# Moving a kernel's gate writes from ScalarE's DMA queue to GpSimd's, spreading gathers over the freed blocks, and loading residual rows later

## The chip, the cores and the metric

One core of a Trainium2 chip. The metric is the device time of one execution in microseconds (us), median over runs. Engines are named as in the profile: PE (TensorE), DVE (VectorE), ACT (ScalarE), POOL (GpSimd), SP (SyncE, which here only issues DMAs). DMAs are issued from three queues: SP's and ACT's (in the profile q1 and q10, "hardware_dynamic") and POOL's (q0, "software_dynamic").

## What is computed

A decoder layer on 1024 tokens of width 1024: a mixer (attention and a diagonal state-space model), cross-attention, and an expert layer. The change touches the expert layer and the final norm alone:

```
q = (h @ w_pq).reshape(b, s, 8, 2, 128)
scores = einsum('bshid,hikd->bshik', q, sub_keys)          # 128 keys per half
half_val, half_idx = top_k(scores, 16)
best_val, best_pos = top_k(all 256 sums, 16)               # 16 experts per head
expert = i1 * 128 + i2                                     # one of 16384
gate = softmax(best_val)
act = einsum('btd,bthkd->bthk', h_blk, peer_u[e_blk])
out = einsum('bthk,bthkd->btd', gate * gelu(act), peer_v[e_blk])
return rmsnorm(h + out, g_final)
```

## The kernel before

Tokens come in 8 blocks of 128 (tb 0 to 7), experts in 128 blocks of 128 (e 0 to 127). Two methods share the work. For tb 3 to 7 (the dense blocks, ND = 5) the kernel multiplies all experts: it needs a dense gate matrix, expert x token, mostly zeros. For tb 0 to 2 it gathers rows of the tables by expert number instead: 128 gathers of 128 rows (512 KB) for each token block and table; tb 2 takes its activations from the dense product and gathers rows of peer_v alone.

**The expert loop** runs e from 0 to 127. `u_load` (L1523) brings 512 KB of peer_u on SP's queue two blocks ahead, `u_hi` (L1529, ACT) and `u_lo` (L1535, DVE) split it into two parts one block ahead, `expert_acts` (L1542) runs 48 matmuls on PE, a GELU on ACT, and writes the result to DRAM with two DMAs on ACT's queue (acm, actd). Into each block other work is put by `plan(e, rank, f)`: all of block e's entries are issued in the order of their rank, and this order is kept by hand on every engine's queue (`in_order`, L1631). `u_hi` has rank -1, `u_lo` and `u_load` 0.5, `expert_acts` 7.

Such work is, first, the **dense gates**. For each dense token block, one after the other with a period of PER = 22 blocks from T0 = 6, the blocks 0 to 16 of the period make the gate matrix in 16 pieces: one-hot rows on DVE (`gate_make`), their scaling on ACT (`gate_power`), 16 small matmuls, and an eviction by ACT into the tile Gs (`gate_mm`, L1505, evicted at L1515). Gs is a single buffer of 64 KB in each partition. `gate_out` (L1517) then writes it to DRAM (gd) in 16 DMAs of 512 KB, each of 8 x 128 pieces of 512 bytes: 4, 3, 3, 3, 3 in the blocks 16 to 20 of the period, rank 4.7, on ACT's queue. The next token block writes Gs again from block 23 on. These five blocks are called a burst here; there are five bursts.

Second, the **gathers**: 384 in the loop. `gather_get` (rank 6) issues one on POOL's queue into one of six buffers, and in the next block (rank 1) `gather_u` (L1319) or `gather_v` (L1334) consumes it on DVE. The list `open_` (L1576) says into which blocks they go, in equal numbers: blocks 13 to 126 without the blocks 17 to 20 of a period, 94 blocks, so four in nearly each and none in the last four blocks of a burst. Third, the **routing** (top-k, expert numbers) of the coming token block, on DVE; in the second and third period two token blocks are routed.

**The last stage** multiplies 32 groups (gi) of four expert blocks. For each expert block `v_load` (L1604) brings a peer_v block, the activations and the gates (vr, vag, gg) on SP's queue into one of two buffers, `v_split` (L1613) scales and splits them on ACT and DVE, and the matmuls of the five dense token blocks (n = 0 to 4) follow. Even n accumulate in PSUM over all groups (`held`), odd n (tb 4 and 6) go through two PSUM buffers that DVE adds to the residual h in every group (`add`, L1670). Gathered rows of tb 1 and 2 are added to h beside it (`take`, L1665). Before the first group, SP's queue gets nine loads: h for all eight token blocks (L1660, 512 KB each) and the final gain (L1662). tb 0, 2, 3, 5 and 7 of h are first used later than the first group.

Of the kernel before, what the change touches and what calls it, by code (L numbers as in the profile page):

```python
# [9 lines left out]
F32 = mybir.dt.float32  # L10
# [13 lines left out]
P = 128  # L24
S = 1024
D = 1024
TB = S // P
# [8 lines left out]
GT_N = 2  # L36
GV_N = 3
# [23 lines left out]
def hybrid_kernel(ctx, tc, x, mem, g_mix, w_in, a_re, a_im, log_dt, b_re, b_im, c_re, c_im, d_skip,  # L61
                  w_glu, b_glu, g_attn, g_ssm, w_out, g_xattn, g_mem, w_xqT, w_xkv, w_xo, g_ffn,
                  g_ffn_row, w_pqT, keysT, peer_uT, peer_u, peer_v, g_final, out, dbg=None, upto=99):
    nc = tc.nc
    V, G = nc.vector, nc.gpsimd
# [897 lines left out]
    with ExitStack() as st:  # L963
# [16 lines left out]
        with ExitStack() as st2:  # L980
# [3 lines left out]
            for th in range(2):  # L984
                t = slice(th * 512, (th + 1) * 512)
# [292 lines left out]
    gd = dr.tile([P, P, TG], F32, name="gd")  # L1278
# [12 lines left out]
    GT, Gs = {}, {}  # L1291
# [14 lines left out]
    def gather(pool, table_ap, tb, k, name, bufs):  # L1306
        r = pool.tile([P, D], F32, name=name, bufs=bufs)
        ins = G.indirect_dma_start(out=r, out_offset=None, in_=table_ap,  # L1308
                                   in_offset=bass.IndirectOffsetOnAxis(ap=gk[tb][0][:, k:k + 1], axis=0))
        return r, ins  # L1310
# [10 lines left out]
    def gather_w(tb):  # L1321
        act(gk[tb][2], gk[tb][2], AF.Gelu_apprx_tanh)
        V.tensor_mul(gk[tb][1], gk[tb][1], gk[tb][2])
# [139 lines left out]
    def plan(e, rank, f):  # L1463
        todo.setdefault(e, []).append((rank, f))
# [34 lines left out]
    def gate_power(tb, b):  # L1499

        o2, power = oneh[tb, b][1], GT[tb][2][0]
        for k in range(8):
            nc.scalar.activation(o2[:, k, :], o2[:, k, :], AF.Copy, scale=power[:, b * 8 + k:b * 8 + k + 1])  # L1503
# [12 lines left out]

    def gate_out(tb, q):  # L1517
        i = slice(q * 8, q * 8 + 8)
        nc.scalar.dma_start(gd[i, :, (tb - GV_N) * P:(tb - GV_N + 1) * P].rearrange("i p t -> p i t"), Gs[tb][:, i, :])

    urows, usplit = {}, {}

# [33 lines left out]
    T0 = 6  # L1556
    PER = 114 // ND
    GSPAN = 16
    R0 = 9
    plan_route(GV_N, 0, 5)  # L1560
    for n in range(ND):
        tb = GV_N + n
        at = T0 + n * PER
        for b in range(16):
            plan(at + b * GSPAN // 16, 0, lambda tb=tb, b=b: gate_make(tb, b))
            plan(at + b * GSPAN // 16, 4.5, lambda tb=tb, b=b: gate_power(tb, b))
            plan(at + b * GSPAN // 16 + 1, 4, lambda tb=tb, b=b: gate_mm(tb, b))
        for q in range(16):
            plan(at + GSPAN + q * 5 // 16, 4.7, lambda tb=tb, q=q: gate_out(tb, q))
        if n + 1 < ND:  # L1570
            r0 = R0 if 0 < n < GV_N else 6
            plan_route(tb + 1, at + r0, PER - 1 - r0)
    for tb in range(GV_N):
        plan_route(tb, T0 + tb * PER, R0 if tb else 6)
    G0 = T0 + 7
    open_ = [e for e in range(G0, P - 1) if (e - T0) % PER not in range(GSPAN + 1, GSPAN + 5)]  # L1576
    V0 = T0 + (ND - 1) * PER + GSPAN + 6

    def v_open():
# [13 lines left out]
    for i, (kind, tb, k) in enumerate(asks):  # L1593
        e = open_[len(open_) * i // len(asks)]
# [58 lines left out]
    with ExitStack() as st:  # L1653
        vpools[1] = st.enter_context(tc.tile_pool(name="vb", bufs=CG, side="right"))
        hp2 = st.enter_context(tc.tile_pool(name="hp2", bufs=1, side="right"))
        psV2 = st.enter_context(tc.tile_pool(name="psV2", bufs=2, space=PSUM))
        psV3 = st.enter_context(tc.tile_pool(name="psV3", bufs=1, space=PSUM))
        h = hp2.tile([P, TB, D], F32, name="hf")
        for tb in range(TB):
            nc.sync.dma_start(h[:, tb, :], h2d[tb])  # L1660
        gfin = hp2.tile([P, D], F32, name="gfin")
        nc.sync.dma_start(gfin, g_final[0:1, :].to_broadcast([P, D]))  # L1662
        got, adds = [], []

        def take(n):  # L1665
            for _ in range(n):
                tb, k, r = got.pop(0)
                V.scalar_tensor_tensor(h[:, tb, :], r, gk[tb][1][:, k:k + 1], h[:, tb, :], op0=OP.mult, op1=OP.add)  # L1668

        def add(n):  # L1670
            for _ in range(n):
                tb, d, pv = adds.pop(0)
                V.tensor_add(h[:, tb, d], h[:, tb, d], pv)  # L1673

        def finish(tb):
            ss = hp2.tile([P, 1], F32, name="ss", bufs=2)
            sq = va_raw.tile([P, D], F32, name="vr")
            nc.scalar.activation(sq, h[:, tb, :], AF.Square, accum_out=ss)
            r = rsqrt_mean(hp2, ss, 1, D, "no")
            V.scalar_tensor_tensor(h[:, tb, :], h[:, tb, :], r, gfin, op0=OP.mult, op1=OP.mult)  # L1680
            nc.sync.dma_start(out[tb * P:(tb + 1) * P, :], h[:, tb, :])

        NG = P // CG
        STEPS = ND
        turn = {math.floor(STEPS * i / CG): i for i in range(CG)}

        held = {n: [psV3.tile([P, 512], F32, name=f"acc{n}{nh}") for nh in range(2)] for n in range(0, STEPS, 2)}
        flat = acm.rearrange("a b (t o) -> (a b t) o", o=1)

        def ask(i):  # L1690

            tb, k = GT_N - 1 + i // P, i % P
            if i < P:
                G.indirect_dma_start(out=gk[GT_N][2][:, k:k + 1], out_offset=None, in_=flat,
                                     in_offset=bass.IndirectOffsetOnAxis(ap=gidx[:, k:k + 1], axis=0))
            if i == P:
                V.tensor_mul(gk[GT_N][1], gk[GT_N][1], gk[GT_N][2])
            got.append((tb, k, gather(hp2, peer_v, tb, k, "rv", 6)[0]))

        NK = (GV_N - GT_N + 1) * P  # L1700
        asked = 0
        with in_order():
            for gi in range(NG):
                for n in range(STEPS):
                    tb = GV_N + n
                    low = None
                    if n in turn and gi + 1 < NG:
                        e = (gi + 1) * CG + turn[n]
                        low = v_split(e)
                        if e + 2 < P:  # L1710
                            v_load(e + 2)
                    if gi == 0 and n == 0:
                        gather_w(GT_N - 1)
                    want = min(NK, NK * (gi * STEPS + n + 1) // ((NG - 1) * STEPS))
                    if len(got) > 3:
                        take(len(got) - 3)
                    while asked < want:
                        if len(got) > 5:
                            take(1)
                        ask(asked)  # L1720
                        asked += 1
                    t = slice(n * P, (n + 1) * P)
                    for nh in range(2):
                        d = slice(nh * 512, nh * 512 + 512)
                        keep = n in held
                        pv = held[n][nh] if keep else psV2.tile([P, 512], F32, name="pv")
                        first, last = not keep or gi == 0, not keep or gi == NG - 1
                        for k, (wh, wl, vh, vl) in enumerate(groups[gi]):
                            mm3(pv, (wh[:, t], wl[:, t]), (vh[:, d], vl[:, d]), first and k == 0, last and k == CG - 1)
                        if last:  # L1730
                            adds.append((tb, d, pv))
                    if n and gi == NG - 1:
                        add(2)
                        finish(tb - 1)
                    else:
                        add(len(adds) - 2 * (n not in held or gi == NG - 1))
                    if low:
                        low()
                groups.pop(gi)
                if gi == NG - 2:  # L1740
                    take(len(got))
                    for tb in range(GV_N):
                        finish(tb)
            tb = TB - 1
            parts = hp2.tile([P, 2], F32, name="parts")
            for k in range(2):
                d = slice(k * 512, k * 512 + 512)
                add(1)
                sq = va_raw.tile([P, D], F32, name="vr")
                nc.scalar.activation(sq[:, d], h[:, tb, d], AF.Square, accum_out=parts[:, k:k + 1])  # L1750
            ss = hp2.tile([P, 1], F32, name="ss", bufs=2)
            V.tensor_add(ss, parts[:, 0:1], parts[:, 1:2])
            r = rsqrt_mean(hp2, ss, 1, D, "no")
            for k in range(2):
                d = slice(k * 512, k * 512 + 512)
                V.scalar_tensor_tensor(h[:, tb, d], h[:, tb, d], r, gfin[:, d], op0=OP.mult, op1=OP.mult)
                nc.sync.dma_start(out[tb * P:(tb + 1) * P, d], h[:, tb, d])
# [57 lines left out]
```

## Time and profile before

| | us |
|---|---|
| median of 3 runs | 3324.71 (3318.75 to 3328.46) |
| profiled execution, its own time | 3330.65 |
| its span | 3328.5 |
| PE busy | 3140.5 (94%) |
| DVE busy | 2554.3 (77%) |
| ACT busy | 1271.5 (38%) |
| POOL busy | 1282.9 (39%) |

Stages: the expert loop runs from 1141 to 2420 us of the span, the last stage from there to the end. How to read the rows below. In a table of stretches: the stretch A:B in us from the span's start and its length, then for PE, PEld (weight load), DVE, ACT and POOL the busy time (and number of instructions), then PE's granted clock as a share of full speed, the mean busy share of the 16 DMA engines, and what they moved in GB/s. The share is a sum of packet durations and can pass 1 a little where packets overlap. In a timeline: start, duration, engine, line, operation, out<-in, count, and in brackets how long the engine was idle before and what ended that. In a view of one line or tile: duration in ns as minimum/median/maximum, then first and last start. In groups of instructions: busy us, mean ns of one | idle time before them and what ended it. An engine's name with a q (ACTq, SPq) is its queue of DMA issues; these do not count as busy.

### The profile page before, as it was taken

The page shows a single profiled execution, that of the slowest core. Times are in us where ns is not written, and L with a number is a line of the kernel's source. Part 1 is how long each engine was busy: PE and PEld are TensorE (multiplying, and loading weights), DVE is VectorE, ACT ScalarE, POOL GpSimd, SP SyncE. Part 2 cuts the span into 40 slices and gives each one's busy share as a digit, 9 for nine tenths or more (in the row PEclk, how much of TensorE's full clock was granted, in tenths as well). Part 3 has the DMA queues.
Part 4 walks back from the last instruction along what each step waited for, and adds up shares of the span by engine and source line. Part 5 has one row for each costly group of instructions (what it writes and reads, how often), then busy time and mean ns, then how long its engine had stood idle before and what let it go on. Part 6 is the DMA issues. An engine that isn't in the chain of part 4 may idle for free.

```text
span 3328.5 us, 46822 instructions
## 1 busy us (share of the span) xinstructions
PE 3140.5 (94%) x16767; PEld 2617.7 (79%) x16767; DVE 2554.3 (77%) x5041; ACT 1271.5 (38%) x2405; POOL 1282.9 (39%) x1099
## 2 busy tenths in 40 slices
PE   7999998999999899998889898999889999999998
PEld 7987675787888688777778787888768888888787
DVE  8356888364588689699699697894768888888887
ACT  3215655154421156365355364562222222222222
POOL 4233545100000005255245254452557777544442
PEclk9999999999999899999999999999989999999999
DMA  5336543531220238988888899899989999898895
GB/s 177 90 91 215 174 136 105 183 114 51 89 92 1 76 105 285 305 271 278 304 269 294 302 329 329 302 332 352 345 309 325 337 334 331 327 341 318 321 335 203
DMA packets 362280, 788.83 MB, mean 237 GB/s; under 512 B 41408, under 2 KB 160704, under 8 KB 358848
## 3 DMA queue, kind: packets, MB, share of 16 engines
q0 software_dynamic: 105056, 356.63, 30.7%
q1 hardware_dynamic: 136928, 336.93, 29.1%
q10 hardware_dynamic: 120064, 92.30, 8.5%
q8 instruction: 131, 2.15, 0.3%
q14 instruction: 101, 0.83, 0.1%
HBM read 649.97 MB, written 135.76 MB: 236 GB/s over the span
## 4 chain that ended last, share of the span: by engine, by line
PE 57%; DVE 19%; issue 10%; DMA 6%; ACT 3%; POOL 2%; ACTq 2%; SPq 1%; DVEq 0%; POOLq 0%
PE pu L1548 12%; DVE ru L1319 4%; PE acc L163 4%; PE acc L162 4%; PE acc L164 4%; PE pp L164 4%; PE pp L162 4%; PE pp L163 4%; DMA gg<-gd 3%; PE pv L162 3%; PE pv L163 3%; PE pv L164 3%; PE pq L162 2%; PE pq L163 2%; PE pq L164 2%
## 5 line engine op out<-in xcount | busy, mean ns | idle before, releaser
L1548 PE MATMUL pu<-hTh,uh 128*128 128x512 f32 (+1 forms) x2048 | 544.1, 347 | 56.9 <-ACT uh L1532 56.8
L1308 POOL DMA_INDIRECT ru<-in_peer_u_dram,ge x256 | 353.8, 1382 | 524.1 <-DVE ru L1319 341.9
L1548 PE MATMUL pu<-hTh,ul 128*128 128x512 f32 (+1 forms) x2048 | 535.4, 343 | 6.3 <-DVE ul L1539 6.3
L1548 PE MATMUL pu<-hTl,uh 128*128 128x512 f32 (+1 forms) x2048 | 534.9, 343 | 0.0
L1308 POOL DMA_INDIRECT rv<-in_peer_v_dram,ge x256 | 361.2, 1411 | 306.5 <-DVE hf L1668 250.9
L1548 PEld LDWEIGHTS pu<-hTh,uh 128*128 128x128 f32 x2048 | 321.2, 193 | 103.7 <-ACT uh L1532 60.8
L1548 PEld LDWEIGHTS pu<-hTh,ul 128*128 128x128 f32 x2048 | 319.9, 192 | 54.7 <-DVE ul L1539 8.5
L1548 PEld LDWEIGHTS pu<-hTl,uh 128*128 128x128 f32 x2048 | 319.8, 192 | 46.2
L1668 DVE SCALAR_TENSOR_TENSOR hf<-rv,gg,hf 128x1024 f32<-128x1024 f32 x256 | 327.7, 1280 | 3.6
L1539 DVE TENSOR_TENSOR ul<-ur,uh 128x1024 fp32r<-128x1024 f32 x128 | 156.3, 1221 | 199.6 <-ACT uh L1532 183.6
L1319 DVE SCALAR_TENSOR_TENSOR ru<-ru,hn 128x1024 f32<-128x1024 f32 x256 | 305.2, 1223 | 1.8 <-DMA ru<-in_peer_u_dram,ge 1.8
L162 PE MATMUL acc<-vh,wh 128*128 128x512 f32 x768 | 298.8, 389 | 0.9 <-issue 0.9
L164 PE MATMUL acc<-vh,wl 128*128 128x512 f32 x768 | 298.8, 389 | 0.0
L163 PE MATMUL acc<-vl,wh 128*128 128x512 f32 x768 | 298.8, 389 | 0.0
L1618 ACT CAST vh<-vr 128x1024 fp32r<-128x1024 f32 x128 | 134.7, 1052 | 363.3 <-PE acc L164 178.1
L1308 POOL DMA_INDIRECT ru<-in_peer_v_dram,ge x128 | 160.9, 1257 | 238.5 <-DVE hf L1334 190.2
L88 ACT ACTIVATE ag<-pu 128x512 f32<-128x512 f32 (+1 forms) x256 | 110.8, 484 | 345.8 <-PE pu L1548 239.0
L1503 ACT ACTIVATE o<-o,power 128x128 bf16<-128x128 bf16 x640 | 194.1, 388 | 104.5 <-DVE o L1492 76.3
L162 PE MATMUL pv<-vh,wh 128*128 128x512 f32 x512 | 201.7, 394 | 20.0 <-DVE hf L1673 20.0
L1621 DVE TENSOR_TENSOR gg<-gg,vag 128x640 f32<-128x640 f32 x128 | 105.8, 826 | 142.6 <-DMA gg<-gd 130.7
L1622 ACT CAST wh<-gg 128x640 fp32r<-128x640 f32 x128 | 93.3, 729 | 303.6 <-DVE gg L1621 254.5
L164 PE MATMUL pv<-vh,wl 128*128 128x512 f32 x512 | 200.7, 392 | 0.0
(496 smaller groups left out, 6931.3 us busy)
## 6 DMA issues: line engine op xcount, KB each, us to landing
ur<-in_peer_uT_dram SPq DMA_DIRECT2D x128, 512.0 KB
vr<-in_peer_v_dram SPq DMA_DIRECT2D x128, 512.0 KB
actd<-ag ACTq DMA_DIRECT2D x128, 320.0 KB
gd<-Gs ACTq DMA_DIRECT2D x80, 512.0 KB
vag<-actd SPq DMA_DIRECT2D x128, 320.0 KB
gg<-gd SPq DMA_DIRECT2D x128, 320.0 KB
qk<-qkd POOLq DMA_DIRECT2D x16, 768.0 KB
wr<-in_w_in_dram SPq DMA_DIRECT2D x8, 1024.0 KB
```

Source lines behind the costliest of these rows:

```text
L88: ins = nc.scalar.activation(o, i, func, **kw).ins
L162: nc.tensor.matmul(out_ap, lh, rh, start=first, stop=False, **kw)
L163: nc.tensor.matmul(out_ap, lh, rl, start=False, stop=False, **kw)
L164: nc.tensor.matmul(out_ap, ll, rh, start=False, stop=last, **kw)
L1308: ins = G.indirect_dma_start(out=r, out_offset=None, in_=table_ap, in_offset=bass.IndirectOffsetOnAxis(ap=gk[tb][0][:, k:k + 1], axis=0))
L1319: V.scalar_tensor_tensor(r, r, 1.0, hn[tb], op0=OP.mult, op1=OP.mult, accum_out=gk[tb][2][:, k:k + 1])
L1503: nc.scalar.activation(o2[:, k, :], o2[:, k, :], AF.Copy, scale=power[:, b * 8 + k:b * 8 + k + 1])
L1539: V.tensor_sub(ul, urows.pop(e), uh.bitcast(F32))
L1548: nc.tensor.matmul(pu[th][:, :b - a], w[:, dc, :], r_[:, dc, a:b], start=f, stop=l)
L1618: nc.scalar.copy(vh, vr)
L1621: V.tensor_mul(gg, gg, ag)
L1668: V.scalar_tensor_tensor(h[:, tb, :], r, gk[tb][1][:, k:k + 1], h[:, tb, :], op0=OP.mult, op1=OP.add)
```

## The change

`gate_out` issues on POOL's queue instead of ACT's, and its rank goes from 4.7 to 6.5, behind the gathers of its block. `open_` now lists every block from 13 to 126: five times, but two times for the blocks 16 to 20 of a period. That makes 495 entries for the same 384 gathers, so about 3.9 gathers in an ordinary block and 1.6 in a block of a burst. In the last stage three loads of h stay ahead of the first group (tb 1, 4, 6); the other five and the final gain follow one by one, at the ends of groups 1 to 6.

```diff
     def gate_out(tb, q):
         i = slice(q * 8, q * 8 + 8)
-        nc.scalar.dma_start(gd[i, :, (tb - GV_N) * P:(tb - GV_N + 1) * P].rearrange("i p t -> p i t"), Gs[tb][:, i, :])
+        G.dma_start(gd[i, :, (tb - GV_N) * P:(tb - GV_N + 1) * P].rearrange("i p t -> p i t"), Gs[tb][:, i, :])
...
         for q in range(16):
-            plan(at + GSPAN + q * 5 // 16, 4.7, lambda tb=tb, q=q: gate_out(tb, q))
+            plan(at + GSPAN + q * 5 // 16, 6.5, lambda tb=tb, q=q: gate_out(tb, q))
...
-    open_ = [e for e in range(G0, P - 1) if (e - T0) % PER not in range(GSPAN + 1, GSPAN + 5)]
+
+    open_ = [e for e in range(G0, P - 1) for _ in range(2 if (e - T0) % PER in range(GSPAN, GSPAN + 5) else 5)]
...
-        for tb in range(TB):
+        gfin = hp2.tile([P, D], F32, name="gfin")
+
+        def h_load(tb):
             nc.sync.dma_start(h[:, tb, :], h2d[tb])
-        gfin = hp2.tile([P, D], F32, name="gfin")
-        nc.sync.dma_start(gfin, g_final[0:1, :].to_broadcast([P, D]))
+
+        soon = [GT_N - 1] + [GV_N + n for n in range(TB - GV_N) if n % 2]
+        for tb in soon:
+            h_load(tb)
+        later = [lambda tb=tb: h_load(tb) for tb in range(TB) if tb not in soon]
+        later.append(lambda: nc.sync.dma_start(gfin, g_final[0:1, :].to_broadcast([P, D])))
...
                 groups.pop(gi)
+                if gi and later:
+                    later.pop(0)()
                 if gi == NG - 2:
```

## Rows read from the trace of the kernel before

**Rows 1.** The page: busy time of the engines, and the software queue.

```profile
PE 3140.5 (94%) x16767; PEld 2617.7 (79%) x16767; DVE 2554.3 (77%) x5041; ACT 1271.5 (38%) x2405; POOL 1282.9 (39%) x1099
...
q0 software_dynamic: 105056, 356.63, 30.7%
```

**Rows 2.** Table of stretches: the five bursts, then two stretches between bursts.

```profile
1336.00:1400.00 64.00, 57.35 (x313) 49.32 (x312) 40.54 (x70) 20.22 (x33) 20.75 (x15) 0.92 1.01 343
1583.00:1646.00 63.00, 53.73 (x293) 46.44 (x292) 37.46 (x67) 16.60 (x24) 17.83 (x12) 0.92 0.99 337
1820.00:1885.00 65.00, 55.40 (x294) 47.40 (x293) 39.18 (x63) 16.63 (x24) 15.70 (x12) 0.92 0.96 324
2024.00:2099.00 75.00, 64.55 (x360) 55.27 (x359) 46.57 (x73) 22.83 (x37) 21.50 (x16) 0.93 0.98 318
2248.00:2305.00 57.00, 53.73 (x294) 45.70 (x293) 16.78 (x18) 13.00 (x20) 9.58 (x8) 0.97 1.02 339
...
1408.00:1583.00 175.00, 158.56 (x1027) 135.55 (x1026) 170.05 (x387) 100.48 (x210) 90.33 (x63) 0.96 0.81 267
...
1885.00:2024.00 139.00, 139.00 (x958) 121.91 (x957) 136.65 (x241) 89.46 (x193) 73.46 (x58) 1.00 0.90 316
```

**Rows 3.** Timeline of ACT at the start of the second burst.

```profile
1583.83 2.06 ACT L1515 ACTIVATE Gs<-pg 128x512 f32<-128x512 f32 x2
1585.93 13.96 ACTq L1519 DMA_DIRECT2D gd<-Gs  x4
1599.92 1.28 ACT L84 ACT_TABLE_LOAD   x1 [14.02 <-issue]
```

**Rows 4.** Timeline of PE in the same burst.

```profile
1605.42 0.80 PE L1548 MATMUL pu<-hTh,uh 128*128 128x512 f32 x1 [6.57 <-ACT uh L1532]
```

**Rows 5.** The tensor gd: its writes, and who waited for them.

```profile
L1519 ACTq DMA_DIRECT2D gd<-Gs x80: 377/1147/10139, 1352.2 to 2293.2; - x80
...
  ACT ag L88: 45.5, 10
```

**Rows 6.** Groups of instructions: what DVE does for one gather.

```profile
L1319 DVE SCALAR_TENSOR_TENSOR ru<-ru,hn 128x1024 f32<-128x1024 f32 x256 | 305.2, 1223 | 1.8 <-DMA ru<-in_peer_u_dram,ge 1.8
...
L1319 DVE DVE_READ_ACCUMULATOR ru<-ru,hn 128x1 f32 x256 | 20.9, 81 | 0.0
```

**Rows 7.** Table of stretches: mostly gate rows; then software copies of 2 KB pieces.

```profile
1384.00:1388.00 4.00, 1.65 (x5) 1.44 (x6) 1.67 (x2) 1.18 (x2) 0.00 (x0) 0.72 1.03 317
...
386.00:392.00 6.00, 4.07 (x19) 2.60 (x18) 6.00 (x11) 5.02 (x12) 4.11 (x7) 1.00 1.23 371
```

**Rows 8.** Views of lines 185 and 1308: POOL's plain copies and its gathers.

```profile
L185 POOL DMA_DIRECT2D qk<-qkd x16: 761/767/982, 254.2 to 524.0; - x16
...
L1308 POOL DMA_INDIRECT ru<-in_peer_u_dram,ge x256: 933/1426/2002, 1255.5 to 2379.7; - x128
```

**Rows 9.** Table of stretches: the start of the last stage, and its steady part.

```profile
2437.00:2452.00 15.00, 0.00 (x0) 0.00 (x0) 1.44 (x3) 1.63 (x2) 2.99 (x4) 0.62 1.02 404
2452.00:2458.00 6.00, 5.96 (x15) 4.72 (x16) 6.00 (x7) 1.81 (x3) 1.35 (x1) 0.54 0.59 205
...
2480.00:2640.00 160.00, 160.00 (x708) 132.48 (x707) 134.74 (x141) 40.57 (x47) 120.36 (x96) 1.00 0.91 328
```

**Rows 10.** Timeline of SP's queue at the start of the last stage.

```profile
2424.93 3.77 SPq L1660 DMA_DIRECT2D hf<-h2d  x8
2428.74 0.92 SPq L1662 DMA_DIRECT2D gfin<-in_g_final_dram  x1
2430.15 0.33 SPq L1606 DMA_DIRECT2D vr<-in_peer_v_dram  x1
```

**Rows 11.** Timelines of DVE and of PE there.

```profile
2450.56 0.82 DVE L1621 TENSOR_TENSOR gg<-gg,vag 128x640 f32<-128x640 f32 x1 [22.97 <-DMA gg<-gd]
...
2452.04 0.79 PE L162 MATMUL pv<-vh,wh 128*128 128x512 f32 x1 [15.05 <-DVE hf L1673]
```

## The prediction

> **What bounds the kernel now.** The page comes first: PE is busy 94% of the span [rows 1], so little can be won except where PE stands or runs at half its clock. The table of stretches shows where that is in the expert loop: in the five bursts, in which gate rows are written, PE is busy 57.35 of 64 us, 53.73 of 63, 55.40 of 65, 64.55 of 75 and 53.73 of 57, and the granted clock is 0.92, 0.92, 0.92, 0.93 and 0.97 [rows 2]. Idle time adds up to 39.2 us. The clock's shortfall times the length of each burst gives 5.1 + 5.0 + 5.2 + 5.3 + 1.7 = 22.3 us more, as an upper end, since part of it falls on idle time. So the bursts hold at most 61 us, and PE's work in them is about 324 - 61 = 263 us.
>
> The timelines say why PE stands. ACT evicts the last piece of Gs, then issues four gate rows, and that holds it for 13.96 us [rows 3]; the split `u_hi` of the next expert block is behind it, and PE waits 6.57 us for that split [rows 4]. Over all 80 issues the median is 1147 ns, the minimum 377 and the maximum 10139; ACT's GELU waited 10 times, 45.5 us in all, until a gate row had landed [rows 5]. A free queue takes an issue in 0.38 us; these are held because the DMA engines are full, with a share of 0.96 to 1.02 in the bursts [rows 2].
>
> Between bursts there are two kinds of stretch. At 1885 PE is busy all the time at full clock. At 1408, in a period that routes two token blocks, DVE is busy 170.05 of 175 us and PE 158.56: DVE is the bound there [rows 2]. At the start of the last stage PE stands for 15.05 us [rows 11] and comes back at a granted clock of 0.54, near the lower of its two levels (1.2 of 2.4 GHz) [rows 9].
>
> **Gate rows to POOL's queue (the main term).** 80 issues leave ACT, which then reaches `u_hi` and the GELU on time. What they cost on POOL: the trace has plain copies there, which took 761 to 982 ns for 384 pieces [rows 8]; a gate row has 1024 pieces. Below, the price is 0.77 us; above, I scale the gather, 0.93 us for 128 pieces [rows 8], by eight: 7.5 us. I take 1 us, since the plain copy is the nearest operation. Sixteen a burst are 16 us; POOL is busy 9.6 to 21.5 us of a burst of 57 to 75 [rows 2], so its idle time hides them. If that cover went, the gathers behind them on POOL's queue would be late, then DVE's `gather_u`, then `u_lo` behind it, then PE.
>
> The bytes do not change, and this is why I don't book all 61 us. The DMA engines' work in the bursts now is the sum of length times share: 64.6 + 62.4 + 62.4 + 73.5 + 58.1 = 321 us. The plan puts about eight gathers into a burst instead of four; one is 512 KB, 1.3 us at 404 GB/s [rows 9]; 4 x 1.3 x 5 = 26 us more, so 347 us, against 263 us of PE work. What saves it is that nobody waits for a gate row at once: Gs is written again from block 23 of the period, two blocks or some 17 us after the burst. Per burst that is 69 us of DMA work against 53 us of PE work and 17 us of delay that costs nothing: it just fits, and the stretch after has room (0.81 or 0.90 share, and four gathers fewer) [rows 2]. But the gathers now stand behind gate rows in the same software queue, and DVE consumes them one block after their issue; POOL's six buffers give it one to two blocks of slack, and what is later than that stops `u_lo`. I leave 4 to 5 us a burst for this and take a gain of 38 us. Bounds: 61 us if nothing is late, nothing if the whole DMA work stays inside the burst: at the share of about 1.07 that such stretches could reach (1.03 with mostly gate rows [rows 7]), 347 / 1.07 = 324 us, as long as now.
>
> The Trainium skill speaks against this part: its page "DMA: Bandwidth & Descriptors", section "Issuing engines are not separate DMA queues", says that all issuing engines' DMAs run on the same 16 engines and that another issuer saves only the issue time, usually small. By that rule alone the gain would be the issue time, and the trace disagrees with "small" here: one set of four issues held ACT 13.96 us [rows 3].
>
> **Gathers thinned outside the bursts.** In the two periods bound by DVE the 16 blocks between bursts lose about 4 gathers each. On DVE one costs 1.223 + 0.081 us [rows 6], so 5.2 us a period, 10 us in all; PE isn't always behind DVE there, so I take 8 (0 to 10). The same gathers come back inside the bursts, where DVE is busy 17 to 47 us of 57 to 75 [rows 2] and hides them.
>
> **Residual rows later.** The loads of h and the final gain go out from 2424.93 to 2429.66, ahead of the first group's vr at 2430.15 [rows 10]. DVE then waits 22.97 us for gg, until 2450.56; the add that frees a PSUM buffer is behind it on DVE, and PE waits 15.05 us for that add [rows 11]. With six of nine loads moved, six issues of 0.47 us and six transfers of 1.3 us (the gain's broadcast counted as one) are no longer ahead: 2.8 + 7.8 = 10.6 us. PE's wait shrinks to about 4.5 us. In the 6 us after the wait PE ran 15 matmuls where the steady rate, 708 in 160 us, gives 26.5 [rows 9]: 2.6 us lost to the lower clock, which a short wait would spare. Gain 13 us; bounds 0 and 17.6, the whole wait and clock loss. The moved loads come one per group, 27 us of PE work with a DMA share of 0.91 [rows 9]: 2.4 us are free in each and one load needs 1.3, so I cost them at nothing; without that cover, 8 us. What is late next is again the v loads, now behind three h loads.
>
> **The sum.** 38 + 8 + 13 = 59 us. Against the profiled execution's own 3330.65 us that is 3272; this execution stands 6 us above the median of the runs, so the forecast for the median is 3266 us.
>
> **The rivals.** *A: the DMA engines keep the bursts as long as they are.* For it: the share of 0.96 to 1.02. Against it: two blocks of delay for the gate rows, and a DMA share of 0.81 to 0.90 right after [rows 2]. Then only 8 + 13 = 21 us are left, 3304 us.
>
> *B, slower: the gate rows come out of the software queue slowly, and the gathers behind them starve DVE.* The fastest that the trace shows software copies together with all else is 371 GB/s in 2 KB pieces [rows 7], 181 pieces per us; that need not be the queue's limit, but if it is, a gate row of 1024 pieces takes 5.7 us. A burst is then 16 x 5.7 + 8 x 1.3 = 102 us, less 17 of free delay 85, against 65 now: 5 x 20 = 100 us lost, 21 gained elsewhere, 3404 us. It decides from 3.9 us a gate row on, where the burst is again 65 us. For it: gathers with DVE working beside them took up to 2002 ns instead of 933 [rows 8]. Against it: the 16 plain copies stayed near 767 ns, and 1024 pieces through ACT's queue need only 524 KB / 308 GB/s = 1.7 us (the rate at share 1) [rows 7]. The Trainium skill has a rule of this kind: "SBUF — State Buffer", section "SBUF: two separate sides", warns that DMAs from GpSimd's queue starve for descriptors while VectorE holds the port that they share; in this trace the gathers agree with it and the plain copies don't.
>
> *C: the last stage doesn't gain.* If the v loads themselves, and not the h loads ahead of them, set the 22.97 us, 46 us are left: 3279 us. For it: gathers run beside them, at a share of 1.02 [rows 9].
>
> **How the numbers follow.** Chances: forecast 0.62, A 0.20, B 0.10, C 0.08. The range goes from all upper ends, 61 + 10 + 17.6 = 89 us, so 3236, over C and A to what A leaves if the last stage gives little, 3316; B is left out. A measurement of this kernel tells 0.3%, 10 us, from no change: faster 0.84, same 0.06 (the slow end of A), slower 0.10 (B).
>
> **What would show it.** Right: no gate issue on ACT; PE busy over 95% in the bursts at a clock near 1.0; bursts of 53 to 60 us; DMA share staying near 1 for 10 to 20 us after them; PE's wait at the start of the last stage under 6 us. Wrong: DVE waiting for gathered rows in or after the bursts, POOL copies of several us each, or `u_hi` waiting for its rows instead of for ACT.

## The result and the profile after

The changed kernel takes 3281.93 us (median of 4 runs, 3275.44 to 3285.88). The kernel before, run beside it, takes 3322.81 us; the ratio is 0.9874, interval 0.9851 to 0.9897. That is 41 us faster, where 59 were forecast: 3281.93 lies in the range, 16 us above the forecast of 3266. The profiled execution took 3284.07 us (span 3282.4, before 3328.5: 46.1 less).

Of the page of the changed kernel: the engines, and the two queues that the change touches (q0 is POOL's software queue, q10 ACT's; packets, MB, and the time of the packets as a share of 16 engines' span).

```profile
PE 3130.6 (95%) x16767; PEld 2612.3 (80%) x16767; DVE 2554.9 (78%) x5041; ACT 1272.6 (39%) x2405; POOL 1343.7 (41%) x1179
...
q0 software_dynamic: 116576, 398.58, 34.9%
...
q10 hardware_dynamic: 36864, 50.35, 4.2%
```

POOL has 80 instructions more than before [rows 1], the gate rows, and is busy 61 us longer.

To see where the time came from, the loop is cut in both kernels where PE starts the first matmul of an expert block, so that the same PE work lies in each piece. (The stretches of [rows 2] were cut by hand around the writes.) A period has 22 blocks: first the table of the five bursts in the changed kernel (blocks 15 to 21 of each period), then of the five blocks after each burst, then the first row and the sum for blocks 5 to 14. Columns as in [rows 2].

```profile
1338.60:1402.30 63.70, 59.75 (x359) 52.13 (x356) 45.77 (x79) 23.64 (x38) 35.43 (x33) 0.99 0.97 333
1562.40:1630.20 67.80, 62.71 (x358) 53.80 (x355) 52.98 (x96) 24.00 (x39) 40.51 (x35) 0.97 0.96 341
1794.10:1859.80 65.70, 61.63 (x359) 52.54 (x356) 53.17 (x86) 23.26 (x39) 37.85 (x35) 1.00 0.98 347
1999.30:2064.20 64.90, 59.77 (x359) 52.46 (x357) 47.43 (x73) 23.64 (x38) 34.86 (x33) 0.99 0.95 328
2206.50:2265.70 59.20, 59.20 (x356) 52.16 (x354) 25.30 (x28) 18.83 (x32) 28.59 (x29) 1.00 0.99 341
sum 321.30, PE 303.06 PEld 263.09 DVE 224.66 ACT 113.36 POOL 177.24; mean PE 60.61 PEld 52.62 DVE 44.93 ACT 22.67 POOL 35.45
...
1630.20:1687.40 57.20, 51.23 (x320) 43.55 (x321) 52.96 (x146) 27.71 (x63) 27.00 (x20) 0.91 0.83 290
...
2265.70:2318.80 53.10, 46.71 (x241) 39.76 (x240) 33.22 (x39) 14.49 (x22) 24.25 (x19) 0.90 0.98 371
sum 255.40, PE 242.99 PEld 210.35 DVE 225.20 ACT 125.79 POOL 124.12; mean PE 48.60 PEld 42.07 DVE 45.04 ACT 25.16 POOL 24.82
...
1245.20:1338.60 93.40, 93.03 (x643) 81.50 (x640) 89.63 (x193) 61.07 (x131) 45.69 (x32) 1.00 0.79 268
...
sum 496.90, PE 477.54 PEld 414.75 DVE 474.16 ACT 312.09 POOL 243.36; mean PE 95.51 PEld 82.95 DVE 94.83 ACT 62.42 POOL 48.67
```

The same cuts in the kernel before: the sum over the bursts, the last row and the sum of the blocks after, the first row and the sum of blocks 5 to 14.

```profile
sum 359.50, PE 319.86 PEld 274.40 DVE 209.17 ACT 108.99 POOL 103.62; mean PE 63.97 PEld 54.88 DVE 41.83 ACT 21.80 POOL 20.72
...
2303.20:2350.10 46.90, 42.63 (x242) 36.74 (x240) 32.96 (x40) 14.38 (x22) 22.11 (x17) 0.98 1.00 379
sum 245.20, PE 233.68 PEld 202.31 DVE 226.89 ACT 129.99 POOL 120.88; mean PE 46.74 PEld 40.46 DVE 45.38 ACT 26.00 POOL 24.18
...
1241.90:1334.90 93.00, 93.00 (x645) 81.63 (x642) 88.48 (x194) 61.10 (x131) 46.15 (x33) 1.00 0.80 272
...
sum 503.50, PE 478.52 PEld 415.48 DVE 483.36 ACT 312.78 POOL 256.85; mean PE 95.70 PEld 83.10 DVE 96.67 ACT 62.56 POOL 51.37
```

So the bursts lost 38.2 us, the five blocks after them grew by 10.2, blocks 5 to 14 lost 6.6. From the end of the last such piece (2350.10 before, 2318.80 after) to the end of the span it is 978.4 and 963.6 us: 14.8 less. The first piece begins 3.3 us later. Together -38.2 + 10.2 - 6.6 - 14.8 + 3.3 = -46.1, the whole difference of the spans. The 10.2 us given back had no term of their own in the forecast: 6.2 of them lie in the last piece alone (46.9 to 53.1). From the end of the last piece on, the 14.8 us hold the blocks 121 to 127 of the loop besides the last stage.

What kind of time it is shows in the sums. In the bursts 21.4 of the 38.2 us are idle time of PE and 16.8 are PE busy shorter for the same matmuls, at a higher clock. In the blocks after, the idle time hardly grew: 9.3 of the 10.2 us are PE busy longer (242.99 against 233.68). The granted clock shows where: it is lower than before in four of the five pieces. Below are the first 5 us after the fourth burst in the changed kernel, then the first 10 in the kernel before. In the changed kernel PE had just stood for 5.1 us (at `pr`, below) and ran at the lower of its two levels; in the kernel before it ran at full clock. That piece grew from 46.5 to 49.3 us.

```profile
2064.20:2069.20 5.00, 5.00 (x16) 4.32 (x17) 4.49 (x12) 1.72 (x6) 1.35 (x2) 0.50 1.02 378
...
2098.00:2108.00 10.00, 9.99 (x68) 8.85 (x69) 9.64 (x18) 4.54 (x12) 2.01 (x2) 1.00 0.26 92
```

What PE waited for there: the waits of PE from 1140 to 2420, first a row of the kernel before, then two of the changed kernel, and then waits of DVE in the changed kernel (us in total, times, longest).

```profile
PE pu L1548 <- ACT uh L1532: 56.8, 11, 15.4
```

```profile
PE pu L1548 <- ACT uh L1532: 28.4, 6, 16.1
...
PE pr L1435 <- DVE i1T L1439: 13.9, 5, 5.1
```

```profile
DVE ru L1319 <- DMA ru<-in_peer_u_dram,ge: 37.8, 19, 4.2
DVE hf L1334 <- DMA ru<-in_peer_v_dram,ge: 17.9, 10, 4.5
```

The wait for `u_hi`, of which [rows 4] showed one, is no longer the bursts' pattern: 16.1 of its 28.4 us are a single wait, at the start of the loop, as the 15.4 were before; without these it fell from 41.4 to 12.3 us. New is `pr` (2.0 us in all before): PE transposes the routing in block 21 of a period and needs a PSUM buffer that DVE empties, and DVE stands in front of gathered rows (1.8 us in the whole kernel before [rows 6], now 37.8). The chain of waits around such a block:

```profile
2025.67 16.93 DMA gd<-Gs
...
2046.15 16.40 DMA ru<-in_peer_u_dram,ge
...
2062.57 1.23 DVE ru L1319 x2
2063.81 0.35 DVE i1T L1439
...
2064.20 0.47 PE pr L1435
```

A gather issued at 2046.15 between gate rows lands 16.40 us later, as late as a gate row; DVE, the copy behind it and PE's transpose follow.

### The profile page after: what moved, and what is told of

It is laid out like the page before. It is cut to its first block, busy times and chain, and to the rows that moved or that the text cites. A ratio compares the mean times of both kernels' runs of the same rounds, so it can differ in the third digit from the quotient of the medians.

```text
span 3282.4 us, 46800 instructions
## 1 busy us (share of the span) xinstructions
PE 3130.6 (95%) x16767; PEld 2612.3 (80%) x16767; DVE 2554.9 (78%) x5041; ACT 1272.6 (39%) x2405; POOL 1343.7 (41%) x1179
## 3 DMA queue, kind: packets, MB, share of 16 engines
q0 software_dynamic: 116576, 398.58, 34.9%
q1 hardware_dynamic: 136928, 336.93, 29.4%
## 4 chain that ended last, share of the span: by engine, by line
PE 54%; DVE 21%; DMA 14%; issue 5%; ACT 3%; POOL 1%; SPq 1%; ACTq 0%; DVEq 0%; POOLq 0%
PE pu L1548 14%; DMA gg<-gd 6%; DVE ru L1319 4%; PE pp L164 4%; PE pp L163 4%; PE pp L162 4%; DMA ru<-in_peer_u_dram,ge 3%; PE acc L164 2%; PE acc L163 2%; PE acc L162 2%; DVE hf L1675 2%; PE pq L162 2%; PE pq L164 2%; PE pq L163 2%; DVE hf L1334 2%
## 5 line engine op out<-in xcount | busy, mean ns | idle before, releaser
L1548 PE MATMUL pu<-hTh,uh 128*128 128x512 f32 (+1 forms) x2048 | 540.6, 345 | 28.4 <-ACT uh L1532 28.4
L1308 POOL DMA_INDIRECT ru<-in_peer_u_dram,ge x256 | 339.2, 1325 | 439.4 <-DVE ru L1319 222.2
L1308 POOL DMA_INDIRECT rv<-in_peer_v_dram,ge x256 | 352.6, 1377 | 295.1 <-DVE hf L1675 240.0
L1548 PEld LDWEIGHTS pu<-hTh,uh 128*128 128x128 f32 x2048 | 319.0, 192 | 73.0 <-ACT uh L1532 30.8
L1319 DVE SCALAR_TENSOR_TENSOR ru<-ru,hn 128x1024 f32<-128x1024 f32 x256 | 306.1, 1224 | 37.8 <-DMA ru<-in_peer_u_dram,ge 37.8
```

The costliest lines, as they stand in the source:

```text
L1319: V.scalar_tensor_tensor(r, r, 1.0, hn[tb], op0=OP.mult, op1=OP.mult, accum_out=gk[tb][2][:, k:k + 1])
L1548: nc.tensor.matmul(pu[th][:, :b - a], w[:, dc, :], r_[:, dc, a:b], start=f, stop=l)
```

## The experiments

The first four divide the change (before, on their chip: 3323.13 us).

**All but the later residual rows.** All nine loads are put back ahead of the first group.

```diff
+        for tb in range(TB):
+            nc.sync.dma_start(h[:, tb, :], h2d[tb])
         gfin = hp2.tile([P, D], F32, name="gfin")
...
-        soon = [GT_N - 1] + [GV_N + n for n in range(TB - GV_N) if n % 2]
-        for tb in soon:
-            h_load(tb)
...
+        nc.sync.dma_start(gfin, g_final[0:1, :].to_broadcast([P, D]))
...
-                if gi and later:
-                    later.pop(0)()
```

> The changed kernel with the loads of h and the final gain as before, all nine ahead of the first group. Theory 1 (each part pays in its own stage; the late loads of h are worth the 13 us that the last stage became shorter): 3295 us, PE waiting about 15 us once at the start of the last stage. Rival (the last stage is shorter only because the expert loop leaves the DMA queues in another state): 3282 us, no such wait.

Measured: 3291.49 us, ratio 0.9900 (0.9881 to 0.9918).

**Only the later residual rows.** Gate rows on ACT's queue, gathers paused as before.

> The kernel before with the later loads of h alone. Theory 1: 3310 us, 13 below before, PE's wait at the start of the last stage 1 to 5 us instead of 15. Rival: no gain that can be told, 3323 us, the wait stays over 10 us because the v loads themselves are late.

Measured: 3309.80 us, ratio 0.9963 (0.9949 to 0.9978): 13.3 us less than before. Both runs give this part 10 to 13 us, and the waits of PE after 2370 say why, first in the run with all nine loads put back, then in the changed kernel:

```profile
PE pv L162 <- DVE hf L1674: 18.9, 3, 14.5
```

```profile
PE pv L162 <- DVE hf L1680: 5.9, 5, 3.3
```

The 15.05 us wait of [rows 11] is there in every kernel with the old loads (14.5 to 15.3 us) and in none with the new (at most 4.0).

**Only the queue.** Gate rows on POOL at rank 6.5, gathers paused, residual rows as before.

> The kernel before with the gate rows on POOL's queue (rank 6.5) alone; gathers pause in the last four blocks of a burst as before. Theory 1 (ACT held by the issues is what made the bursts long, and what was given back right after each burst comes from gathers that stand behind gate rows): bursts of 60 to 65 us, fewer late blocks after them than in the changed kernel, 3290 to 3300 us. Rival (the DVE time of the gathers is what counts, the queue hardly): 3315 to 3323 us.

Measured: 3295.50 us, ratio 0.9911 (0.9894 to 0.9929): 27.6 us. Its sums over the bursts and over the blocks after, cut as above:

```profile
sum 321.20, PE 309.15 PEld 266.52 DVE 210.01 ACT 109.30 POOL 162.20; mean PE 61.83 PEld 53.30 DVE 42.00 ACT 21.86 POOL 32.44
...
sum 254.40, PE 237.94 PEld 205.71 DVE 225.22 ACT 130.16 POOL 116.69; mean PE 47.59 PEld 41.14 DVE 45.04 ACT 26.03 POOL 23.34
```

(Its profiled execution stood 8 us above the median.) So the queue alone takes 38.3 us out of the bursts and gives back 9.2 behind them, as the whole change does. The give-back hardly shrank, though the gathers pause and DVE waits only 10.2 + 5.0 us for gathered rows: on this point theory 1 was wrong, since gathers behind gate rows are not the only source of it.

**Only the thinning.** Gate rows on ACT, residual rows as before, the new `open_`.

> The kernel before with the new list of blocks for the gathers alone; gate rows stay on ACT's queue. Theory 1: the bursts stay as long as before or grow by some us each (four more gathers in a full DMA), the two periods bound by DVE lose 5 us each: 3315 to 3330 us. Rival (thinning is what counts): 3290 to 3300 us.

Measured: 3310.88 us, ratio 0.9955 (0.9939 to 0.9971): 12.2 us. Its profiled execution has 7.1 us less in blocks 5 to 14 (sum 496.40), as the changed kernel, and 11.5 us less in the bursts, which was not expected; the block with four gate rows has fewer gathers beside them now, and that may be why:

```profile
sum 348.00, PE 314.65 PEld 269.69 DVE 222.63 ACT 111.66 POOL 117.25; mean PE 62.93 PEld 53.94 DVE 44.53 ACT 22.33 POOL 23.45
```

The parts alone add up to 53 us; together they give 41. The next four ask where the 12 go (before, on their chip: 3319.66 us).

**Queue and residual rows, without the thinning.**

```diff
-    open_ = [e for e in range(G0, P - 1) for _ in range(2 if (e - T0) % PER in range(GSPAN, GSPAN + 5) else 5)]
+    open_ = [e for e in range(G0, P - 1) if (e - T0) % PER not in range(GSPAN + 1, GSPAN + 5)]
```

> The changed kernel with the old pause of the gathers in the bursts instead of the thinning: gate rows on POOL and later residual rows alone. If the thinning is worth by the side of the queue what it was alone (12 us), 3292 to 3297. Theory 1 (thinned gathers go behind the gate rows, come late, and give back in the five blocks after a burst about what they win outside): 3280 to 3287, with DVE's waits for gathered rows under 20 us and blocks 5 to 14 of the periods some 6 us longer than in the changed kernel.

Measured: 3278.90 us against 3319.66 on its chip, ratio 0.9873 (0.9854 to 0.9891): the same as the changed kernel. Beside the queue the thinning is worth nothing that a median shows, and the details are as theory 1 had them: DVE waits 9.7 + 5.7 us for gathered rows, and blocks 5 to 14 take 503.6 us. (The profiled execution took 3291.64 us, the slowest of the four by 11.) Its bursts and the blocks after, in sum:

```profile
sum 321.00, PE 308.19 PEld 265.50 DVE 209.55 ACT 109.24 POOL 163.69; mean PE 61.64 PEld 53.10 DVE 41.91 ACT 21.85 POOL 32.74
...
sum 254.00, PE 236.28 PEld 203.82 DVE 224.11 ACT 130.72 POOL 118.54; mean PE 47.26 PEld 40.76 DVE 44.82 ACT 26.14 POOL 23.71
```

That is 575 us against 576.7 in the changed kernel, though a burst has about four gathers instead of eight, all in its first block, and PE waits 2.0 us at the transposes. So late gathers are not what keeps these pieces from getting shorter. They fill time that is lost without them to something else, DVE's `u_lo` among it (11.8 us of PE's waits here, 4.0 in the changed kernel).

**Routing ended two blocks earlier.**

```diff
-            plan_route(tb + 1, at + r0, PER - 1 - r0)
+            plan_route(tb + 1, at + r0, PER - 3 - r0)
```

> The changed kernel with the routing of the next token block ended two expert blocks earlier in each period, so that its transposes on PE fall in the middle of a burst and not in the blocks where DVE waits for gathered rows that stand behind gate rows. Theory 1 (the give-back after a burst comes from late gathers, which hold DVE, and so the copies behind the routing's transposes on PE): PE's wait for DVE at the transposes falls from 13.9 us to under 4, the five blocks after the bursts from 272 us to under 264, time 3270 to 3278. Rival 2 (the backlog of gate rows on the DMA engines makes these blocks long whatever DVE does): the wait goes elsewhere, time 3279 to 3286 as the changed kernel.

Measured: 3284.54 us, ratio 0.9896 (0.9874 to 0.9918), no gain. (The 272 us of the expectation count blocks from ACT's `u_hi`; by that cut the blocks after fell to 261 as expected and the bursts grew by 17.) PE's wait at the transposes fell to 7.1 us, not under 4. By the cut used here bursts and blocks after are 318.9 + 260.2 = 579 us, as long as before the edit, and blocks 5 to 14 grew from 496.9 to 503.0. The rival's number came out.

**Gathered rows taken a block later.** What is issued in the blocks 16 to 19 of a period is used by DVE two blocks later.

```diff
-        plan(e + 1, 1, lambda kind=kind, tb=tb, k=k: (gather_u if kind == "u" else gather_v)(tb, k))
+        late = e + 1 + ((e - T0) % PER in range(GSPAN, GSPAN + 4))
+        plan(late, 1, lambda kind=kind, tb=tb, k=k: (gather_u if kind == "u" else gather_v)(tb, k))
         if i == P - 1:
-            plan(e + 1, 1, lambda: gather_w(0))
-            plan(e + 2, 1, early_open)
+            plan(e + 2, 1, lambda: gather_w(0))
+            plan(e + 3, 1, early_open)
...
```

> The changed kernel with gathered rows of the blocks 16 to 19 of a period taken by DVE two blocks after their issue instead of one. Theory 1 (late gathers hold DVE and through it PE): DVE's waits for gathered rows (L1319 and L1334, 38 + 18 us) fall to under half, time 3266 to 3276. Rival 2 (the backlog of gate rows itself): DVE's waits fall too, but PE's don't, time 3279 to 3286.

Measured: 3287.07 us, ratio 0.9902 (0.9883 to 0.9921). This run tells the theories apart badly: DVE's waits fell only to 30.8 + 13.6 us, and since two blocks' gathers are now used right ahead of the transposes, PE's wait there doubled to 28.8 us. Its bursts grew to 331.9 us and the blocks after fell to 250.8.

**Gate rows on SP's queue.**

```diff
-        G.dma_start(gd[i, ...
+        nc.sync.dma_start(gd[i, ...
```

> The changed kernel with the gate rows issued by SP instead of POOL. Theory 3 (an issue waits for the DMA that stands eight before it on the queues that SP and ACT share, whoever issues; POOL's queue has eight of its own): SP is held 10 to 14 us a block in the bursts, the u rows behind come late, u_hi waits for its rows, time 3295 to 3340. Rival (any queue but ACT's does it, since only ACT had something behind the issues that PE needs at once): u rows are loaded two blocks ahead and have the slack, time 3275 to 3290.

Measured: 3290.34 us, ratio 0.9915 (0.9899 to 0.9931): 8 us behind POOL's queue (12 if each is set against the kernel before on its own chip), just above the rival's range and below that of theory 3. Below are the page's row of SP's queue, the issues in the view of gd, two rows of ACT's waits from 1140 to 2420, and the sum over the bursts.

```profile
q1 hardware_dynamic: 220128, 378.88, 33.6%
...
L1519 SPq DMA_DIRECT2D gd<-Gs x80: 377/1610/7226, 1352.8 to 2276.5; - x80
...
ACT uh L1532 <- DMA ur<-in_peer_uT_dram: 105.9, 20, 14.7
...
ACT uh L1532 <- DMA gd<-Gs: 37.0, 4, 12.9
...
sum 342.70, PE 315.23 PEld 269.82 DVE 224.88 ACT 108.36 POOL 117.85; mean PE 63.05 PEld 53.96 DVE 44.98 ACT 21.67 POOL 23.57
```

An issue holds SP for 1610 ns in the median and up to 7226, the u rows behind are late, and ACT's split waits 105.9 us for them (34.7 in the changed kernel): the bursts stay 21 us longer than with POOL. So theory 3's waits are there, only smaller than it put them. Nor is ACT relieved here: it waits 37.0 us for gate rows that SP has issued. The run therefore does not say what relieving ACT alone would be worth; it shows that a queue with the u rows behind it is the worse place. That POOL's queue is better because nothing behind it is urgent is not shown by itself, since that queue also carries the rows in fewer packets (last section). The Trainium skill, "DMA: Bandwidth & Descriptors", section "Issuing engines are not separate DMA queues", counts only the issue time as gain of another issuer; here that time differs, at most 982 ns on POOL against 7226 on SP and 10139 on ACT, and so do the packets.

The last four try to beat the changed kernel (before on their chips: 3321.29 and, for the last, 3321.92).

**The last stage opened two blocks later.** In the changed kernel the first read-backs of gate rows are issued by SP in block 116 (the third row is SP's, the first two ACT's timeline):

```profile
2283.34 0.33 ACTq L1552 DMA_DIRECT2D acm<-ag  x1
...
2285.59 1.04 ACT L1532 CAST uh<-ur 128x1024 fp32r<-128x1024 f32 x1 [10.46 <-DMA gg<-gd]
```

```profile
2274.93 0.51 SPq L1611 DMA_DIRECT2D gg<-gd  x1
```

ACT's GELU is done at 2275, but its store `acm` goes out at 2283.34 and `u_hi` after that.

```diff
-    V0 = T0 + (ND - 1) * PER + GSPAN + 6
+    V0 = T0 + (ND - 1) * PER + GSPAN + 8
```

> The changed kernel with the opening of the last stage's buffers and its first loads (v rows, activations, gate rows read back) two expert blocks later, at block 118 instead of 116. Theory 4 (the first read-backs gg wait until the last gate rows have landed, which the software queue now brings later, and until then they keep ACT's stores of activations, and behind them u_hi, from being issued): ACT's idle time before u_hi put down to gg (10.5 us) and PE's 4 us behind it go, the blocks 116 to 120 fall from 53 us to 44 to 48, time 3273 to 3279. Rival (six loads beside gathers are too many wherever they begin): the same wait two blocks later, time 3279 to 3286.

Measured: 3277.57 us, ratio 0.9865 (0.9846 to 0.9884). The blocks 116 to 120:

```profile
2265.00:2311.60 46.60, 42.16 (x242) 36.49 (x240) 28.18 (x32) 11.22 (x18) 22.06 (x19) 1.00 0.97 370
```

53.1 us have become 46.6, as long as before the change, in the expected range like the time, and the stretch behind them is no longer for it (3276.1 - 2311.6 = 964.5 us against 963.6). The 6.2 us given back in that piece were the last stage's first loads meeting the late gate rows. In the medians the 4 us to the changed kernel lie within the intervals.

**Gathers ahead of most gate rows.**

```diff
-    open_ = [e for e in range(G0, P - 1) for _ in range(2 if (e - T0) % PER in range(GSPAN, GSPAN + 5) else 5)]
+    few = {GSPAN: 3, GSPAN + 1: 3, GSPAN + 2: 3, GSPAN + 3: 0, GSPAN + 4: 0}
+    open_ = [e for e in range(G0, P - 1) for _ in range(few.get((e - T0) % PER, 5))]
```

> The changed kernel with the gathers of a burst put ahead of most of its gate rows: weights 3, 3, 3, 0, 0 instead of 2 in each of the five blocks, so that no gather stands behind the last six gate rows and none is taken by DVE in the block of the routing's transposes. Theory 1 (late gathers hold DVE, the copy of the transposes behind them, and PE): PE's wait at the transposes falls from 13.9 us to under 4, block 21 of the periods 0 to 3 from 10 to 14 us each to about 9, the sum of bursts and five blocks after from 577 us to 562 to 570, time 3268 to 3277. Rival 2 (the backlog on the DMA engines): the blocks 18 to 20 or those after grow by what block 21 loses, time 3279 to 3286.

Measured: 3276.76 us, ratio 0.9869 (0.9847 to 0.9891). PE's wait at the transposes, then the sums of bursts and of blocks after:

```profile
PE pr L1435 <- DVE i1T L1439: 2.0, 5, 0.4
...
sum 320.50, PE 307.75 PEld 265.85 DVE 224.59 ACT 109.05 POOL 175.37; mean PE 61.55 PEld 53.17 DVE 44.92 ACT 21.81 POOL 35.07
...
sum 252.30, PE 235.28 PEld 203.19 DVE 219.21 ACT 131.23 POOL 112.45; mean PE 47.06 PEld 40.64 DVE 43.84 ACT 26.25 POOL 22.49
```

The wait went, as theory 1 said, but the pieces lost only 4 us of the 7 to 15 that it asked for. PE is busy 4.7 us longer in the bursts for the same matmuls, and its waits for `u_lo` grew to 11.4 us. The time lies at the upper end of theory 1's range, the pieces above theirs.

**Both.**

> Both of the two: later opening of the last stage and gathers ahead of most gate rows. If theories 1 and 4 hold and their waits lie in different blocks, the two gains add up: 3261 to 3272, faster than the changed kernel by 10 us or more. If neither holds, 3279 to 3286.

Measured: 3276.35 us, ratio 0.9871 (0.9853 to 0.9889). The time lies outside both forecasts: the two gains did not add up in the median, though its pieces are the shortest so far (317.7 + 247.7 us).

**Both, and fewer gathers in the two periods that route two token blocks.**

```diff
+    def weight(e):
+        n, b = divmod(e - T0, PER)
+        return few.get(b, 4 if n in (1, 2) and b < GSPAN - 1 else 5)
...
```

> The kernel with both (last stage opened at block 118, gathers ahead of most gate rows), and besides fewer gathers in the blocks 0 to 14 of the two periods that route two token blocks (weight 4 instead of 5: about 17 gathers, 23 us of DVE work, go to the other periods). Theory 5 (DVE bounds these two periods, so that a gather moved out of them is worth its 1.3 us, while the other periods have PE as the bound): their blocks 0 to 14, 171 + 166 us with both, fall by 15 to 23 us, the other periods grow by under 6 us, time 3260 to 3270. Rival (all of DVE is as full elsewhere, 0.93 to 0.98 of the time, and what leaves one period comes back in another): 3272 to 3280.

Measured: 3273.11 us (3264.91 to 3281.20), ratio 0.9855 (0.9833 to 0.9877), the lowest median of all, but above the 3260 to 3270 expected and within the rival's range; it is 9 us below the changed kernel, and the two intervals overlap. Blocks 5 to 14 of the two periods, and of the one after:

```profile
1450.90:1556.80 105.90, 98.42 (x643) 84.55 (x641) 102.23 (x222) 65.45 (x134) 46.12 (x33) 0.95 0.79 254
1679.20:1781.80 102.60, 97.98 (x643) 85.46 (x642) 97.59 (x193) 65.86 (x135) 41.07 (x31) 0.95 0.76 250
1890.70:1986.10 95.40, 94.04 (x645) 81.83 (x642) 93.96 (x184) 62.02 (x131) 52.20 (x42) 1.00 0.94 325
```

With both edits alone the three are 113.1, 107.2 and 92.9 us. (The 171 us of the expectation was a slip: the first period's blocks 0 to 14 are 164 with both.) Blocks 0 to 14 of the two periods lost 14 us, just under the 15 expected, and the next one gave back 2.5. In the profile the blocks thus do what theory 5 says. The profiled execution, at 3266.43 us, is one of the two shortest of five, and in the medians the 3 us to the kernel with both are not told from nothing, so the gain in time is not shown.

## Why the prediction was right, and by how much it was off

**Gate rows: right in the bursts, mis-sized in sum.** 38 us were taken and 38.2 are what the bursts lost. That these agree so closely is partly luck: 23 of 61 us were left for late gathers, but the queue alone, with the gathers paused, lost the same 38.3, so what is left in the bursts is mostly something else. The term that was mis-sized is "I leave 4 to 5 us a burst for this and take a gain of 38 us": lateness was to be paid inside that figure, yet it came on top, 10.2 us in the blocks after, nearly all of it PE busy longer at a lower clock. DVE waiting for gathered rows, named as a sign of being wrong, did come (37.8 + 17.9 us, before 1.8 + 3.5). In the profile the net is 28 us, and the run of the queue alone gives 27.6. Six of the ten are a collision that the working did not look for: the read-backs of gate rows in block 116, which was given no cost because "nobody waits for a gate row at once". The last burst has such a reader, and the run that moves it shows so.

**POOL's price: right.** The view of gd in the changed kernel, its issues and what POOL waited for before them:

```profile
L1519 POOL DMA_DIRECT2D gd<-Gs x80: 885/905/982, 1355.1 to 2256.0; - x80
...
  DMA gd<-Gs: 22.2, 19
  ACT Gs L1515: 14.1, 3
  DMA ru<-in_peer_u_dram,ge: 13.2, 10
```

905 ns against 1 us taken; the upper bound of 7.5 us was far off. ACT's GELU, which waited 45.5 us for gate rows to land [rows 5], no longer waits for them. The prediction said that issues are held because the DMA engines are full; but POOL's 80 stay under 1 us at a DMA share of 0.95 to 0.99, so a full DMA alone does not hold an issue. Not foreseen: POOL waits for earlier transfers to land before it issues more. That spaces the gate rows, and with them the gathers behind, as in the chain above.

**PE in the bursts: nearly.** Busy 303.06 of 321.3 us, 94% where over 95 was asked, the clock 0.97 to 1.00 as expected. The bursts are 7.6 us shorter each, as the term says. In the first 10 us after each the DMA share was 0.97 to 1.02, as forecast, and in the next 10 it was 0.81 to 0.97.

**Thinning: the mechanism right, the sum wrong.** Blocks 5 to 14 lost 6.6 us (8 taken). But without the thinning the kernel is as fast (3278.90), so this term adds nothing that the runs can measure; alone, without the queue, it gave 12.2, most of it likewise unlooked for, in the bursts. Why 6.6 us in the profile don't show in the medians stays open: the term is as large as the intervals are wide to either side (0.2%, 7 us), and single executions of one kernel scatter by 6 to 22 us.

**Last stage: right, slightly small.** 13 us taken; 14.8 in the profile, 13.3 alone, 9.6 taken out. The wait fell from 15.05 to 3.3 us (4.5 expected), and the moved loads cost nothing that shows.

**The sum.** Against 59 forecast, the profile has 10 less for the gate rows, 1.4 less for the thinning, 1.8 more for the last stage and 3.3 less for a later start of the loop: 46. The medians differ by 41 to 43, since the profiled execution before stood 6 us above its median and the one after 2.

**The rivals.** A fell with the bursts' length, though something of it is true: bursts and blocks after together came down by only 28 of 605 us, at a DMA share of 0.95 to 0.99 in the bursts. The share of 1.07, on which the lower bound of the gain rests, shows in none of these. B fell with POOL's 905 ns. The rule beside it, in the Trainium skill's "SBUF — State Buffer", section "SBUF: two separate sides", starves the DMAs of GpSimd's queue only while VectorE holds the port that they share; the 80 issues show no sign of it, within 885 to 982 ns with DVE busy 70% of the bursts. Its price was also worked out from 1024 pieces a gate row, which is not how that queue carries them (below); and by its own terms it would decide from 4.5 us a gate row on ((65 + 17 - 8 x 1.3) / 16), not from 3.9. C fell with the last stage.

**Open.** What still holds bursts and blocks after at 565 to 583 us in every variant on POOL's queue, where five times the last burst's 59.2 us alone would be 296 instead of 321, was not settled: taking away single waits (the transposes', the gathered rows', the read-backs') moved 0 to 11 us.

## What to carry to other kernels

Before a transfer that nobody needs soon is moved, look at what stands behind it on the new queue: on SP's the u rows came late, and the bursts stayed 21 us longer than with POOL's. Book what comes late after the move as a cost of its own, in the stretch behind, and look for the one reader that does come soon, at the end of a loop above all. Parts that relieve the same stretch don't add up, so cost them in the order in which they take effect.

## What was not expected of the hardware

The software queue carries a gate row in fewer, larger packets. Its 80 rows add 116576 - 105056 = 11520 packets and 41.9 MB to q0 ([rows 1] and the page above): 144 packets a row, 3.6 KB each on average. With SP issuing the same rows, q1 has 220128 packets against 136928 in the changed kernel's page, 1040 a row:

```profile
q1 hardware_dynamic: 136928, 336.93, 29.4%
```

It also carries them in less of the DMA engines' time. ACT's queue in the page of the kernel before:

```profile
q10 hardware_dynamic: 120064, 92.30, 8.5%
```

Shares times spans, before and after, give an estimate for the 80 rows: 124 us on POOL's queue (34.9% of 3282.4 less 30.7% of 3328.5) against 145 us on ACT's (8.5% of 3328.5 less 4.2% of 3282.4). So up to some 20 us of what the queue alone brought can be cheaper transfers and not the relief of ACT; no run tells the two apart.

And an engine's issue can be held by a transfer that another engine issued: ACT's stores waited for SP's loads of the last stage to land (10.46 us), as POOL's gate rows waited for POOL's own earlier transfers. The trace's records name what they wait for. In the loop the DMAs of SP and ACT share eight semaphores (the counters that tell a landing) and POOL's have eight others; ACT's store at 2283.34 comes after a wait for the semaphore that SP's load at 2274.46 had taken. So this wait is one that the built program asks for. Another number of semaphores was not tried.
